# Rotary embedding on one core: a small zero write to the output, placed behind the load of batch 3

## The chip, the core and the metric

The kernel runs on one core of one Trainium2 chip. The metric is the device time of one execution in microseconds (us); lower is better. Three runs of the kernel before gave 317.55, 317.91 and 318.12 us, so its median is 317.91 us.

## What is computed

The reference applies a rotary position embedding. For each of 8 batches, 2048 positions and 16 heads, a row of 64 numbers is cut into two halves, which are rotated by the position's cosine and sine:

```python
x1 = x[..., :head_dim // 2].copy()
x2 = x[..., head_dim // 2:].copy()
...
out1 = x1 * cos - x2 * sin
out2 = x1 * sin + x2 * cos
return np.concatenate([out1, out2], axis=-1).astype(np.float32)
```

Input `x` and output have the shape (8, 2048, 16, 64) in float32, which is 8.39 MB for each batch and direction. `cos` and `sin` have 2048 rows of 32 numbers.

## The kernel before, in words

**Tiling.** One batch is one tile `xt` of 128 partitions with 16 positions (J = 16) of 16 heads of 64 numbers, so partition p holds positions 16p to 16p+15. In memory a partition's part of a batch is one contiguous piece of 64 KB. In SBUF the tile is float16 (32 KB a partition). The cast lies in the DMAs: `load` (L48) reads float32 and writes float16, `store` (L57) reads float16 and writes float32. Both are issued from GpSimd (POOL), and all of them go through one queue, q0 in the profile, in the order in which POOL issues them. I call the load of batch b "load b" and its store "store b".

**Buffers.** The pool `rope_io` has five buffers (NBUF, L27). Loads 0 to 4 are issued at once at the start (L74). Load 5 takes the buffer of batch 0 and waits until store 0 has landed; load 6 waits for store 1, and load 7 for store 2.

**Arithmetic.** `rotate` (L62) is four VectorE (DVE) instructions for each batch, at L67, L68, L70 and L72: two products into a scratch tile `v`, one product in place in `xt`, one sum in place. The store of a batch waits for its L72.

**Start.** The first two positions of batch 0 come in float32 through SyncE (SP) into `head` (L36), which the ScalarE (ACT) casts into the tile at L75. SP also loads `sin_f` (L45) and `cos_f` (L46), and ACT makes the float16 tables from them (L79, L80, L81). The DMAs from SP go through another queue, q1 in the profile.

**End.** The store of batch 7 is cut into three parts: 9 positions at L95 (`gate`), 5 positions at L97 (`rest`), both from POOL, and the last 2 positions through ACT's cast at L105 and a DMA from SP at L106, which waits for `gate` to land.

**What sets the order.** The program's scheduler puts POOL's DMAs in this order: loads 0 to 4, stores 0 and 1, loads 5 and 6, stores 2 and 3, load 7, stores 4, 5 and 6, `gate`, `rest`. POOL runs in order: when one of these waits, all that follow it wait. The ACT engine's order is L75, L79, L80, L81 and then, at the end of the kernel, L105. A helper, `add_manual_dep`, adds a dependency between two instructions by hand; with `Sync` the later one waits on a semaphore until the earlier one is done, and for a DMA this means that it has landed.

Of the kernel before, what the change touches and what calls it, by code (L numbers as in the profile page):

```python
# [1 line left out]

# [4 lines left out]


@with_exitstack  # L10
def kernel(
    ctx: ExitStack,
    tc: tile.TileContext,
    x: bass.AP,
    cos: bass.AP,
    sin: bass.AP,
    out: bass.AP,
):
    nc = tc.nc
    f16 = mybir.dt.float16  # L20
    f32 = mybir.dt.float32

    B, S, H, D = x.shape
    Dh = D // 2
    P = nc.NUM_PARTITIONS
    J = S // P
    NBUF = 5  # L27

    const_pool = ctx.enter_context(tc.tile_pool(name="rope_const", bufs=1))
    io_pool = ctx.enter_context(tc.tile_pool(name="rope_io", bufs=NBUF))  # L30
    tmp_pool = ctx.enter_context(tc.tile_pool(name="rope_tmp", bufs=1))

    JA = 2
    head = const_pool.tile([P, JA, H, D], f32)
    x0 = x[0].rearrange("(p j) h d -> p j (h d)", j=J)
    nc.sync.dma_start(  # L36
        out=head.rearrange("p j h d -> p (j h d)"),
        in_=x0[:, 0:JA, :].rearrange("p j f -> p (j f)"),
    )
    sin_f = const_pool.tile([P, J, Dh], f32)  # L40
    cos_f = const_pool.tile([P, J, Dh], f32)
    cos_h = const_pool.tile([P, J, Dh], f16)
    sin_h = const_pool.tile([P, J, Dh], f16)
    neg_h = const_pool.tile([P, J, Dh], f16)
    nc.sync.dma_start(out=sin_f, in_=sin.rearrange("(p j) d -> p j d", j=J))  # L45
    nc.sync.dma_start(out=cos_f, in_=cos.rearrange("(p j) d -> p j d", j=J))  # L46

    def load(b):  # L48
        xt = io_pool.tile([P, J, H, D], f16)
        j0 = JA if b == 0 else 0  # L50
        nc.gpsimd.dma_start(  # L51
            out=xt[:, j0:J, :, :].rearrange("p j h d -> p (j h d)"),
            in_=x[b].rearrange("(p j) h d -> p j (h d)", j=J)[:, j0:J, :].rearrange("p j f -> p (j f)"),
        )
        return xt

    def store(b, xt):  # L57
        nc.gpsimd.dma_start(  # L58
            out=out[b].rearrange("(p j) h d -> p (j h d)", j=J), in_=xt
        )  # L60

    def rotate(xt):  # L62
        v = tmp_pool.tile([P, J, H, D], f16)
        sin_b = sin_h.unsqueeze(2).to_broadcast([P, J, H, Dh])
        neg_b = neg_h.unsqueeze(2).to_broadcast([P, J, H, Dh])
        cos_b = cos_h.unsqueeze(2).to_broadcast([P, J, 2 * H, Dh])
        nc.vector.tensor_mul(out=v[:, :, :, 0:Dh], in0=xt[:, :, :, Dh:D], in1=neg_b)  # L67
        nc.vector.tensor_mul(out=v[:, :, :, Dh:D], in0=xt[:, :, :, 0:Dh], in1=sin_b)  # L68
        xw = xt.rearrange("p j h (e d) -> p j (h e) d", d=Dh)
        nc.vector.tensor_mul(out=xw, in0=xw, in1=cos_b)  # L70
        xa = xt.rearrange("p j h d -> p (j h d)")
        nc.vector.tensor_add(out=xa, in0=xa, in1=v.rearrange("p j h d -> p (j h d)"))  # L72

    tiles = [load(b) for b in range(NBUF)]  # L74
    nc.scalar.copy(  # L75
        out=tiles[0][:, 0:JA, :, :].rearrange("p j h d -> p (j h d)"),
        in_=head.rearrange("p j h d -> p (j h d)"),
    )
    nc.scalar.copy(out=sin_h, in_=sin_f)  # L79
    nc.scalar.mul(out=neg_h, in_=sin_f, mul=-1.0)  # L80
    nc.scalar.copy(out=cos_h, in_=cos_f)  # L81
    def part(b, j0, j1):
        return (
            out[b].rearrange("(p j) h d -> p j (h d)", j=J)[:, j0:j1, :].rearrange("p j f -> p (j f)"),
            tiles[b][:, j0:j1, :, :].rearrange("p j h d -> p (j h d)"),
        )

    for b in range(B):
        rotate(tiles[b])
        if b < B - 1:  # L90
            store(b, tiles[b])
        if b + NBUF < B:
            tiles.append(load(b + NBUF))
    dst, src = part(B - 1, 0, 9)
    gate = nc.gpsimd.dma_start(out=dst, in_=src)  # L95
    dst, src = part(B - 1, 9, J - JA)
    rest = nc.gpsimd.dma_start(out=dst, in_=src)  # L97
    tc.add_manual_dep(
        rest.ins,
        gate.ins.name,  # L100
        mybir.DependencyInfo(mybir.DependencyClass.NoSync, mybir.DependencyReason.DATA),
        reason="order of the ring",
    )
    dst, src = part(B - 1, J - JA, J)
    nc.scalar.copy(out=head.rearrange("p j h d -> p (j h d)"), in_=src)  # L105
    end = nc.sync.dma_start(out=dst, in_=head.rearrange("p j h d -> p (j h d)"))  # L106
    tc.add_manual_dep(
        end.ins,
        gate.ins.name,
        mybir.DependencyInfo(mybir.DependencyClass.Sync, mybir.DependencyReason.DATA),  # L110
        reason="the last rows go out behind this part",
    )


# [1 line left out]
_INS = ['x', 'cos', 'sin']  # L116
_OUTS = [((8, 2048, 16, 64), 'float32')]


# [23 lines left out]
```

## Time and profile before

| quantity | value |
|---|---|
| median of three runs | 317.91 us |
| time of the profiled execution | 317.42 us |
| its span, first to last instruction | 315.6 us |
| time outside of the span | 1.82 us |
| DVE busy | 209.2 us (66%) |
| ACT busy | 6.8 us (2%) |
| POOL busy | 9.4 us (3%) |
| read from HBM, written to HBM | 67.63 MB, 67.11 MB |

The table is from the page of the profiled execution. The span is the time from the first to the last instruction of the core; what lies outside of it is the difference between the profiled execution's own time and its span. A DMA's issue appears on the engine that issues it (POOLq and SPq are the sequencers' own rows) and takes about half a microsecond; the transfer itself runs later on the 16 DMA engines. Each DMA of 128 partitions appears there as 128 data packets, 8 for each DMA engine, and 16 packets of 4 bytes, one for each engine, which report completion. The profile counts a transfer by the bytes at its destination: a load of a batch counts 4.19 MB, a store 8.39 MB, though both have 8.39 MB on their HBM side.

### The profile page before, as it was taken

Reading aid. Unit: us, or ns where it says so; the run is one execution under the profiler, and the core shown is the slowest. Engines: PE = TensorE matmul, PEld = TensorE weight load, DVE = VectorE, ACT = ScalarE, POOL = GpSimd, SP = SyncE. Lnnn points to the kernel's source line nnn. Section 1 sums busy time; section 2 is a strip of 40 time slices with the busy share of each in tenths; the row PEclk is TensorE's granted clock in tenths of the full one; section 3 lists DMA queues with packets and bytes.
Section 4 is the critical chain, followed back from the end, with each engine's and each line's share of the span. In section 5 each row is a group of like instructions: output and inputs, shape, how many; then the busy total and the mean of one; then the engine's idle time right before and its main releaser. Section 6 shows DMA issues by size and latency. Waiting matters only on the chain.

```text
span 315.6 us, 126 instructions
## 1 busy us (share of the span) xinstructions
DVE 209.2 (66%) x32; ACT 6.8 (2%) x6; POOL 9.4 (3%) x21
## 2 busy tenths in 40 slices
DVE  0009599999999999999979999990009994000000
ACT  4010000000000000000000000000000002000000
POOL 3000000000000000010000000100000001000000
DMA  9899999999999999999999999999999999999998
GB/s 278 184 261 207 200 249 216 199 199 249 216 199 266 399 424 507 399 332 233 233 199 199 390 407 399 399 532 266 199 224 507 399 399 498 432 399 399 432 424 341
DMA packets 3024, 101.71 MB, mean 322 GB/s; under 512 B 336, under 2 KB 336, under 8 KB 592
## 3 DMA queue, kind: packets, MB, share of 16 engines
q0 software_dynamic: 2448, 99.09, 98.0%
q1 hardware_dynamic: 576, 2.62, 2.2%
HBM read 67.63 MB, written 67.11 MB: 427 GB/s over the span
## 4 chain that ended last, share of the span: by engine, by line
issue 25%; DMA 23%; DVE 21%; another core or an unknown queue 13%; POOL 1%; ACT 1%; SPq 0%; POOLq 0%; DVEq 0%; ACTq 0%
DMA xt<-in_x_dram 12%; DMA cos_f<-in_cos_dram 11%; DVE xt L70 8%; DVE xt L72 8%; DVE v L68 3%; DVE v L67 1%; ACT head L105 1%; POOL out_dram L58 1%; POOL xt L51 0%; ACT cos_h L81 0%; SPq L45 0%; SPq L36 0%; POOLq L58 0%; DVEq L67 0%
## 5 line engine op out<-in xcount | busy, mean ns | idle before, releaser
L70 DVE TENSOR_TENSOR xt<-xt,cos_h 128x16384 f16<-128x16384 f16 x8 | 69.5, 8692 | 4.2 <-ACT cos_h L81 3.9
L72 DVE TENSOR_TENSOR xt<-xt,v 128x16384 f16<-128x16384 f16 x8 | 69.5, 8692 | 0.3
L67 DVE TENSOR_TENSOR v<-xt,neg_h 128x8192 f16<-128x8192 f16 x8 | 35.4, 4425 | 50.1 <-DMA xt<-in_x_dram 49.9
L68 DVE TENSOR_TENSOR v<-xt,sin_h 128x8192 f16<-128x8192 f16 x8 | 35.3, 4417 | 0.0
L51 POOL DMA_DIRECT2D xt<-in_x_dram x8 | 4.4, 560 | 117.1 <-DMA out_dram<-xt 116.3
L105 ACT CAST head<-xt 128x2048 f32<-128x2048 f16 x1 | 1.9, 1897 | 227.6 <-DVE xt L72 227.6
L58 POOL DMA_DIRECT2D out_dram<-xt x7 | 3.7, 535 | 87.8 <-DVE xt L72 87.8
L95 POOL DMA_DIRECT2D out_dram<-xt x1 | 0.5, 531 | 50.5 <-DVE xt L72 50.5
L75 ACT CAST xt<-head 128x2048 f16<-128x2048 f32 x1 | 1.9, 1898 | 3.4 <-DMA head<-in_x_dram 3.4
L75 ACT ACT_TABLE_LOAD x1 | 1.3, 1283 | 0.7 <-PEq L127 0.7
L81 ACT CAST cos_h<-cos_f 128x512 f16<-128x512 f32 x1 | 0.6, 617 | 18.0 <-DMA cos_f<-in_cos_dram 18.0
L79 ACT CAST sin_h<-sin_f 128x512 f16<-128x512 f32 x1 | 0.6, 617 | 9.1 <-DMA sin_f<-in_sin_dram 9.1
L80 ACT ACTIVATE neg_h<-sin_f 128x512 f16<-128x512 f32 x1 | 0.6, 624 | 0.0
L97 POOL DMA_DIRECT2D out_dram<-xt x1 | 0.5, 531 | 0.0
L127 POOL MEMSET const-float32-0.0<- 128x1 f32 x1 | 0.1, 98 | 0.2 <-issue 0.2
L127 POOL MEMSET const-bfloat16-1.0<- 128x1 bf16 x1 | 0.1, 101 | 0.0
L127 POOL MEMSET const-float32-1.0<- 128x1 f32 x1 | 0.1, 98 | 0.0
L127 POOL MEMSET const-uint8-127<- 128x1 uint8 x1 | 0.1, 98 | 0.0
## 6 DMA issues: line engine op xcount, KB each, us to landing
xt<-in_x_dram POOLq DMA_DIRECT2D x7, 4096.0 KB, 41.1
out_dram<-xt POOLq DMA_DIRECT2D x1, 4608.0 KB, 42.3
xt<-in_x_dram POOLq DMA_DIRECT2D x1, 3584.0 KB, 22.2
out_dram<-xt POOLq DMA_DIRECT2D x1, 2560.0 KB, 47.9
head<-in_x_dram SPq DMA_DIRECT2D x1, 1024.0 KB, 4.7
out_dram<-head SPq DMA_DIRECT2D x1, 1024.0 KB, 8.4
sin_f<-in_sin_dram SPq DMA_DIRECT2D x1, 256.0 KB, 15.2
cos_f<-in_cos_dram SPq DMA_DIRECT2D x1, 256.0 KB, 33.9
```

The lines of the kernel that those rows point to most:

```text
L51: nc.gpsimd.dma_start(out=xt[:, j0:J, :, :].rearrange("p j h d -> p (j h d)"), in_=x[b].rearrange("(p j) h d -> p j (h d)", j=J)[:, j0:J, ...
L58: nc.gpsimd.dma_start(out=out[b].rearrange("(p j) h d -> p (j h d)", j=J), in_=xt)
L67: nc.vector.tensor_mul(out=v[:, :, :, 0:Dh], in0=xt[:, :, :, Dh:D], in1=neg_b)
L68: nc.vector.tensor_mul(out=v[:, :, :, Dh:D], in0=xt[:, :, :, 0:Dh], in1=sin_b)
L70: nc.vector.tensor_mul(out=xw, in0=xw, in1=cos_b)
L72: nc.vector.tensor_add(out=xa, in0=xa, in1=v.rearrange("p j h d -> p (j h d)"))
L75: nc.scalar.copy(out=tiles[0][:, 0:JA, :, :].rearrange("p j h d -> p (j h d)"), in_=head.rearrange("p j h d -> p (j h d)"),)
L79: nc.scalar.copy(out=sin_h, in_=sin_f)
L80: nc.scalar.mul(out=neg_h, in_=sin_f, mul=-1.0)
L81: nc.scalar.copy(out=cos_h, in_=cos_f)
L95: gate = nc.gpsimd.dma_start(out=dst, in_=src)
L105: nc.scalar.copy(out=head.rearrange("p j h d -> p (j h d)"), in_=src)
```

## The change

A tile of 128 partitions with 128 float32 zeros each (512 bytes) is made with a memset on POOL. A DMA that the ACT queue issues writes it to the output: in each partition's 64 KB piece of batch 0, to the first 512 bytes. By a dependency made by hand the DMA waits until load 3 has landed. Store 0 later writes the same bytes with the result. Since both write to the same place, the tile framework orders them. The built program's list of waits shows it: in it, store 0 waits for the DMA from ACT to land, besides the waits that it had before. In that program the memset stands on POOL behind loads 0 to 4 and ahead of store 0, and the DMA stands on ACT behind the cast of `cos_h` and ahead of the cast of L105 (L119 in the changed file). The order of all other instructions on each engine is the same.

```diff
@@ -45,13 +45,16 @@
+    loads = []
+
     def load(b):
         xt = io_pool.tile([P, J, H, D], f16)
         j0 = JA if b == 0 else 0
-        nc.gpsimd.dma_start(
+        dma = nc.gpsimd.dma_start(
             out=xt[:, j0:J, :, :].rearrange("p j h d -> p (j h d)"),
             in_=x[b].rearrange("(p j) h d -> p j (h d)", j=J)[:, j0:J, :].rearrange("p j f -> p (j f)"),
         )
+        loads.append(dma)
         return xt
@@ -79,6 +82,17 @@
     nc.scalar.copy(out=cos_h, in_=cos_f)
+    zero = const_pool.tile([P, 128], f32)
+    nc.gpsimd.memset(zero, 0.0)
+    blank = nc.scalar.dma_start(
+        out=out[0].rearrange("(p j) h d -> p (j h d)", j=J)[:, 0:128], in_=zero
+    )
+    tc.add_manual_dep(
+        blank.ins,
+        loads[3].ins.name,
+        mybir.DependencyInfo(mybir.DependencyClass.Sync, mybir.DependencyReason.DATA),
+        reason="a first write behind this load",
+    )
```

## The prediction, made before the changed kernel was run

> **What bounds the kernel now.** I read the page first: the busy shares, the row of DMA in 40 slices, and the queues.
>
> ```profile
> DVE 209.2 (66%) x32; ACT 6.8 (2%) x6; POOL 9.4 (3%) x21
> ...
> DMA  9899999999999999999999999999999999999998
> ...
> q0 software_dynamic: 2448, 99.09, 98.0%
> ...
> HBM read 67.63 MB, written 67.11 MB: 427 GB/s over the span
> ```
>
> No compute engine is the bound: DVE is busy for 66% of the span. The 16 DMA engines are busy in every slice, and POOL's queue q0 alone takes 98.0% of their time. So the end is set by one stream of transfers without a gap. A gap made anywhere in it moves everything behind it, and nothing later can take it back.
>
> Second I read the timeline around the place that is changed, for what is issued when.
>
> ```profile
> 0.74 0.38 SPq L36 DMA_DIRECT2D head<-in_x_dram  x1
> ...
> 1.25 2.79 POOL L51 DMA_DIRECT2D xt<-in_x_dram  x5 [0.80 <-PEq L138]
> ...
> 35.55 0.62 ACT L81 CAST cos_h<-cos_f 128x512 f16<-128x512 f32 x1 [17.98 <-DMA cos_f<-in_cos_dram]
> ...
> 54.18 0.54 POOL L58 DMA_DIRECT2D out_dram<-xt  x1 [50.14 <-DVE xt L72]
> ...
> 80.15 0.54 POOL L58 DMA_DIRECT2D out_dram<-xt  x1 [25.43 <-DVE xt L72]
> ...
> 121.83 0.53 POOL L51 DMA_DIRECT2D xt<-in_x_dram  x1 [41.14 <-DMA out_dram<-xt]
> ```
>
> Store 0 is issued at 54.18, store 1 at 80.15. Third, the DMA view of two short windows, one around the issue of load 3 (2.95) and one around that of load 4 (3.47), gives the time to landing:
>
> ```profile
> xt<-in_x_dram POOLq DMA_DIRECT2D x1, 4096.0 KB, 78.8
> ```
> ```profile
> xt<-in_x_dram POOLq DMA_DIRECT2D x1, 4096.0 KB, 98.7
> ```
>
> Load 3 lands at 2.95 + 78.8 = 81.7, load 4 at 3.47 + 98.7 = 102.2. So store 0 stands in the queue 48 us before the loads are through, and follows load 4 without a pause: its first packets start at 101.47 to 101.85 in the packet records (101.66 in the middle).
>
> Fourth, the last packets of load 4. The DMA view of 95.7 to 98.1 us and that of 98.1 to 101.4 us hold one packet of 32 KB for each engine:
>
> ```profile
> q0 software_dynamic: 16, 0.52, 101.4%
> ```
> ```profile
> q0 software_dynamic: 16, 0.52, 99.5%
> ```
>
> The first share means 1.014 x 2.4 = 2.43 us for a packet, the second 0.995 x 3.3 = 3.28 us. The engines lose 0.85 us here, just ahead of the run's first write to HBM; no other q0 packet of the trace takes over 2.6 us. This is what a first write placed earlier could move.
>
> **What the Trainium skill says.** The page "DMA: Bandwidth & Descriptors" bears on this in four places.
> - Section "Queues, rings and completion order": each DMA engine takes turns between the queues that have work, one packet at a time. Between 7.2 and 23.4 us the trace agrees: the two queues finish as many packets as each other, though q1's are small, and `cos_f` takes 33.9 us to land.
>
> ```profile
> q0 software_dynamic: 144, 3.74, 107.1%
> q1 hardware_dynamic: 144, 0.26, 4.8%
> ```
>
>  At the end the trace does not: L106 is issued at 306.36, but from 306.4 to 311.5 us only q0 has packets, and q1's start at 311.55 when q0 is empty.
>
> ```profile
> q0 software_dynamic: 107, 2.19, 104.0%
> ```
>
>  A DMA that comes to a filled queue may thus also have to wait for what is in it.
> - Section "Specifications": about 1 us to the first byte for a DMA from GpSimd, 0.6 us for one from SP or ACT. For SP the trace has 1.0 us (L36 at 0.74, first packets at 1.74). For POOL it has one case with an idle queue, the start: issue at 1.25, first q0 packet at 5.10, 3.85 us, which may be long because five issues stand together and `head` is on the engines.
> - Section "Anatomy of one DMA — SWDGE (gpsimd) path": a wait for a semaphore is done by the issuing sequencer before dispatch. The trace agrees: L51 at 121.83 follows the landing of store 0 (54.18 + 67.4 = 121.6) by 0.28 us.
> - Section "Issuing engines are not separate DMA queues": the ACT queue has no engines of its own. Here the SP queue's packets are on the same 16.
>
> **The change, part by part.**
> 1. *Memset on POOL.* 128 elements a partition behind the five load issues. The memsets of one element take 0.1 us; I take 0.1 to 0.3 us near 4 us. POOL then has nothing to do until 54.18. Cost 0. Without that cover it would be the 0.1 to 0.3 us.
> 2. *The wait on ACT.* ACT stands at the DMA from 36.2 (end of L81) until load 3 lands at 81.7. Behind it on ACT there is only the cast for the tail, which ran at 263.77, and nobody else waits for that. Cost 0; the cover is 180 us long.
> 3. *The zeros' transfer.* Issue about 81.8, ready for the engines 1.0 us later (the measured lead of L36), at 82.8. Load 4 has just begun, with 8 packets for each engine from 81.1 on, 2.43 us each. The zeros are also 8 packets for each engine. If the queues take turns, the first goes behind load 4's first packet, the eighth behind its eighth, at 102.1. A 2 KB packet of `sin_f` stretched the time from one load packet to the next from 2.13 to 2.21, so 512 bytes cost about 0.03 us each, 0.25 us in all. If the zeros must wait for what is queued, as at the tail, they start when load 4 ends. Either way they end when load 4 ends.
> 4. *The 0.85 us stall.* Taking turns, it comes under one of load 4's early packets, as long as before: no gain, and load 4 still ends at about 101.9. Waiting behind load 4, the load ends 0.85 us sooner and the zeros pay the stall: the same sum. At best it is hidden: minus 0.85. At worst it is paid by the zeros and by store 0 again: plus 0.85. I take 0.
> 5. *When the zeros have landed.* The last packet of a store ends 0.42 us before the landing is seen (store 0: completion packets up to 121.13, landing 121.55). That gives 102.1 + 0.42 = 102.5 with turns, and 102.7 without (101.0 + 0.85 + 8 x 0.05 + 0.42). I take 102.6.
> 6. *The new wait on store 0.* POOL reacts 0.28 us after a landing: issue at 102.9. From a POOL issue to its first packet the cost is 1.0 us by the skill, 3.85 us by the start of this trace. I take 1.8, which lies nearer the lower end because here one DMA is issued into idle engines. First packet at 104.7. Before, it was at 101.66. The gap is 3.0 us, from 2.2 to 5.1 by the lead alone. The first packets of `head` on idle engines took 0.43 to 0.94 instead of 0.31 us, so I add 0.1: 3.1 us.
> 7. *What stands behind store 0 on POOL.* Store 1, ready at 79.87, is issued half a microsecond behind it at about 103.4, far ahead of its turn at 124. Load 5 waits for the landing of store 0, while store 1 is on the engines for 19.3 us, so there is no second gap. Load 6, stores 2 and 3, load 7 and the rest follow in the same way, each 3.1 us later. DVE's wait ahead of batch 5 grows from 1.59 to 4.7 us, and its 209.2 us still fit.
>
> Sum: 0 + 0 + 3.1 = 3.1 us. From the profiled execution's own time, 317.42 + 3.1 = 320.5 us (span 318.7). The median of the runs lies 0.49 us above that execution, and I forecast on its scale: 317.91 + 3.1 = 321.0 us.
>
> **The rivals.**
> - *The zeros land early.* If an engine takes several of the 512-byte packets in one turn, four or more at once, they land before about 99. Store 0's issue (0.28 + 1.8 us) is then done before load 4 ends, and no gap opens. The point is 99.5: landing before it costs nothing. Place: inside load 4. If the 0.85 us stall is then hidden under load 4's reading, the time is 317.91 - 0.85 = 317.1, faster; if it holds load 4 up, 317.9. For it: the packets are small. Against it: `sin_f` and `cos_f` got one packet a turn, and the tail's DMA not even that.
> - *The lead of a POOL issue into idle engines is that of the start.* 102.9 + 3.85 = 106.8, and store 0 pays the 0.85 us as well: 5.1 + 0.85 = 6.0, hence 323.9 us. For it: the only idle start in the trace. Against it: five issues stood together there.
> - *The change doesn't do what it says*, because store 0 is not held back at run time, say because all semaphores are up before: 317.9. Against it: the list of waits of the built program has store 0 waiting on the landing of the zeros.
>
> **How the numbers follow.** Forecast 0.80 (time 319.2 to 323.2: from lead 1.0 with the stall hidden, 2.2 - 0.85, about +1.3, to lead 3.85, about +5.2). Early landing 0.10, half of it faster. Lead and stall both full 0.07. No effect 0.03. The range of 319.0 to 323.2 leaves out early landing, no effect and most of the third case, just under 2 in 10. A measurement of this kernel can tell about 0.2%, or 0.64 us, from no change. Faster: 0.05. Same: the other half of early landing and no effect, 0.08. Slower: 0.87.
>
> **What would show it.** Store 0's issue must move from 54.18 to about 102.9, with POOL's wait ahead of it ended by the DMA of the zeros, and store 1's must follow at once. The DMA row must have a hole of 2 to 5 us at 102 to 105, the only one. The stall of 3.28 us must move off load 4's last packet. Load 5 must be issued at about 125 instead of 121.83, and all after it shifted by the same amount. If store 0 is issued before 99, steps 3 and 6 are wrong; if the hole is there but the span does not grow by it, step 7 is.

## The result, and the profile after

The changed kernel takes 319.49 us in the median (318.87 to 319.90, 6 runs) against 317.94 us for the kernel before (317.36 to 318.12, 6 runs). The ratio is 1.0052 with a 95% interval of 1.0037 to 1.0067: slower by 1.55 us, where 3.1 were forecast. The profiled execution took 319.21 us with a span of 317.4 us; the spans differ by 1.8 us.

From the page of the kernel after, the lines that answer to those shown of before:

```profile
DVE 209.2 (66%) x32; ACT 6.8 (2%) x6; POOL 9.6 (3%) x22
...
DMA  9899999999996999999999999999999999999998
...
q0 software_dynamic: 2448, 99.09, 97.2%
...
q10 hardware_dynamic: 144, 0.07, 0.1%
HBM read 67.63 MB, written 67.17 MB: 425 GB/s over the span
```

The row of DMA has one new digit, a 6 in the 13th slice (95.2 to 103.2 us). Everything else is as full as before. q10 is the ACT queue: 128 data packets and 16 completion packets, 0.07 MB, 0.1% of the engines' time. What it moves takes next to nothing of the engines' time; what is new beside it is the hole.

The timeline of after around that slice, and the row of its view of waits that is new (engine, line, what it waited for: us in total, times, longest):

```profile
81.99 0.37 ACTq L87 DMA_DIRECT2D out_dram<-zero  x1
...
102.40 1.06 POOL L61 DMA_DIRECT2D out_dram<-xt  x2 [98.14 <-DMA out_dram<-zero]
...
123.67 0.53 POOL L53 DMA_DIRECT2D xt<-in_x_dram  x1 [20.20 <-DMA out_dram<-xt]
```
```profile
POOL out_dram L61 <- DMA out_dram<-zero: 98.1, 1, 98.1
```

The zeros are issued at 81.99, when load 3 has landed. Store 0 is issued at 102.40 in place of 54.18, released by the zeros, with store 1 right behind it. Load 5 is issued at 123.67 in place of 121.83, 1.84 us later, and that shift stays until the end. The windows view of after shows the hole (columns: the stretch, its length, busy time of DVE, ACT and POOL, clock, DMA share, GB/s):

```profile
98.00:100.00 2.00, 2.00 (x1) 0.00 (x0) 0.00 (x0) 1.00 1.24 266
100.00:102.00 2.00, 2.00 (x1) 0.00 (x0) 0.00 (x0) 1.00 0.04 9
102.00:104.00 2.00, 2.00 (x1) 0.00 (x0) 1.06 (x2) 1.00 1.22 524
104.00:106.00 2.00, 2.00 (x1) 0.00 (x0) 0.00 (x0) 1.00 0.99 426
```

A packet is counted where it starts, so a share over 1 reaches into the stretch behind it, and the hole lies from about 101 to 103.5 us. In the packet records load 4's data ends at 100.8 to 101.3, the zeros' last packets at 101.36, and store 0's first packets start at 103.51. The DMA view of 98.2 to 100.8 us has load 4's last packets:

```profile
q0 software_dynamic: 16, 0.52, 93.9%
q10 hardware_dynamic: 16, 0.01, 1.5%
```

0.939 x 2.6 = 2.44 us a packet: the stall of 0.85 us, which the kernel before has here and which I call "the loss" from here on, is gone, and no other load packet of after takes over 2.65 us. So the trace has two opposite terms. Means over 16 packets, one for each engine: load 4's last packets start at 98.54 (before: 98.36), so their usual 2.43 us end at 100.97; store 0's first start at 103.57 (before: 101.64). 2.60 us of gap, less 0.85 us of loss, plus 0.18 us by which load 4 is later, are the 1.93 us between 101.64 and 103.57.

### The profile page after: what moved, and what is told of

Its sections match the earlier page's. It is cut to its first block, busy times and chain, and to the rows that moved or that the text cites. A ratio compares the mean times of both kernels' runs of the same rounds, so it can differ in the third digit from the quotient of the medians.

```text
span 317.4 us, 131 instructions
## 1 busy us (share of the span) xinstructions
DVE 209.2 (66%) x32; ACT 6.8 (2%) x6; POOL 9.6 (3%) x22
## 4 chain that ended last, share of the span: by engine, by line
DMA 36%; issue 25%; another core or an unknown queue 14%; DVE 7%; ACT 1%; POOL 1%; SPq 0%; POOLq 0%; ACTq 0%; DVEq 0%
DMA xt<-in_x_dram 12%; DMA cos_f<-in_cos_dram 11%; DMA out_dram<-xt 7%; DMA out_dram<-zero 6%; DVE xt L75 3%; DVE xt L73 3%; DVE v L71 1%; ACT head L119 1%; POOL xt L53 0%; POOL out_dram L61 0%; ACT cos_h L84 0%; SPq L45 0%; SPq L36 0%; DVE v L70 0%
## 5 line engine op out<-in xcount | busy, mean ns | idle before, releaser
L70 DVE TENSOR_TENSOR v<-xt,neg_h 128x8192 f16<-128x8192 f16 x8 | 35.4, 4425 | 52.4 <-DMA xt<-in_x_dram 52.2
L119 ACT CAST head<-xt 128x2048 f32<-128x2048 f16 x1 | 1.9, 1897 | 229.4 <-DVE xt L75 229.4
```

## The experiments

Two things were open: why the loss of 0.85 us went away, and whether the gap is made as the prediction says. In all times, "before" is the kernel before, timed beside the experiment on the same chip. The lengths of packets are means over the 16 packets, one for each engine, of the one profiled execution.

**The zeros to another batch (e1_batch4).**

```diff
-        out=out[0].rearrange("(p j) h d -> p (j h d)", j=J)[:, 0:128], in_=zero
+        out=out[4].rearrange("(p j) h d -> p (j h d)", j=J)[:, 0:128], in_=zero
```

> The zeros go to the rows of batch 4 in place of batch 0, still behind load 3; store 0 is free of them, and store 4, which overwrites them, is issued 100 us after they land. My theory (the 0.85 us belong to the run's first write to HBM, and a small write takes them over unseen; the loss of the change is the gap of 2.15 us ahead of store 0): no gap, no packet of load 4 over 2.6 us, 317.1 us, about 0.8 us faster than before. Rival (the 0.85 us belong to the pass from loads to stores in a filled queue, and went away only because the queue was empty): no gap, load 4's last packet again 3.3 us, 317.9 us, as before.

317.71 us, before 317.79; ratio 0.9999 (0.9990 to 1.0007). Store 0 is issued at 51.96, the gap is gone, and with it the whole cost of the change. But load 4's last packets are long again, in the DMA view of 98.4 to 101.4 us:

```profile
q0 software_dynamic: 16, 0.52, 100.2%
```

1.002 x 3.0 = 3.01 us a packet. My theory fell: the zeros did not take the loss over.

**The zeros early (e2_load1).**

```diff
-        loads[3].ins.name,
+        loads[1].ins.name,
```

> As the change, with the zeros behind load 1 in place of load 3. They should land at 62 to 66 us and store 0 be issued then, 35 us before load 4 ends. First-write theory: no gap, no long packet, 317.1 us. Filled-queue rival: no gap, load 4's last packet 3.3 us, 317.9 us. A third view, in which it's the ACT queue itself that costs (a further queue to set up or to wait for at the end): over 318 us without any gap.

317.77 us, before 317.79; ratio 0.9998 (0.9991 to 1.0006). All 128 rows of zeros landed at 67.7, store 0 was issued at 68.28, no gap, and load 4's last packets are still long, in the DMA view of 98.6 to 101.4 us:

```profile
q0 software_dynamic: 16, 0.52, 104.1%
```

1.041 x 2.8 = 2.91 us a packet. So the loss doesn't belong to the run's first write to HBM, nor to the first write to these pieces of batch 0. The ACT queue itself costs nothing that can be measured, and neither does the wait on store 0 when it ends this early.

**No zeros, store 0 held until load 4 has landed (e3_hold).**

```diff
+            if b == 0:
+                tc.add_manual_dep(
+                    put.ins,
+                    loads[4].ins.name,
...
```

> No zeros; store 0 waits by hand for load 4 to land. This makes the gap without an early write. Both: load 4's last packet 2.43 us, landing about 101.3, issue about 101.9, first packets about 103.0. First-write theory: store 0 itself is then held up by about 0.85 us (long first packets or a landing that late), so the span grows by 2.2 us to about 317.8, 320.1 us. Filled-queue rival: no stall, the span grows by 1.4 us, 319.3 us.

318.77 us, before 317.79; ratio 1.0030 (1.0018 to 1.0041), 0.98 us slower. The timeline of e3_hold:

```profile
101.90 1.07 POOL L61 DMA_DIRECT2D out_dram<-xt  x2 [97.86 <-DMA xt<-in_x_dram]
```

Load 4's last packets took 2.43 us; store 0's first packets started at 103.07 in the mean and took 2.43 us, too. In both kernels in which store 0 comes to an empty queue, with the zeros and without, it pays no loss. The gap alone makes this kernel slower. It costs less than in the changed kernel, as load 4 lands at 101.32 here and the zeros land at 101.81 there, so store 0 is issued 0.50 us earlier.

**One packet for each engine in place of eight (e4_16rows).**

```diff
-        out=out[0].rearrange("(p j) h d -> p (j h d)", j=J)[:, 0:128], in_=zero
+        out=out[0].rearrange("(p j) h d -> p (j h d)", j=J)[0:16, 0:128], in_=zero[0:16, :]
```

> As the change, but only 16 of the 128 rows of zeros are written, so each DMA engine has one packet in place of eight. If the eight turns of one packet each are what carries the landing to 101.8, the zeros land at about 86.5 now, store 0 is issued at 87 and the gap is gone. First-write theory: 317.1 us. Filled-queue rival: 317.9 us. If the landing is set by something else than the turns, the gap stays and the time is near 319.5 us.

317.83 us, before 317.79; ratio 1.0001 (0.9992 to 1.0010). The timeline of e4_16rows, and the DMA view of its 97.9 to 101.3 us:

```profile
82.30 0.37 ACTq L87 DMA_DIRECT2D out_dram<-zero  x1
91.73 1.07 POOL L61 DMA_DIRECT2D out_dram<-xt  x2 [87.47 <-DMA out_dram<-zero]
```
```profile
q0 software_dynamic: 17, 0.52, 99.5%
```

The turns are what carries the landing: in the packet records the zeros' data start at 85.9 on 14 engines and at 88.4 on two, the completion packets one load packet later, at 88.4 and 90.8. They land at 91.1. I had expected 86.5, since I had counted neither the completion packet's own turn nor that two engines might join a packet later. There is no gap, but the loss is back (3.38 us in the mean; the 17th packet in the view is a completion packet of 4 bytes), though store 0 was issued as late as 91.73.

**The kernel before again (e5_before).** No edit.

> The kernel before, once more, for a second profile. If the loss ahead of store 0 belongs to the kernel and not to one execution, load 4's last packets are long again, by 0.5 to 0.95 us (the four cases so far: 0.85, 0.62, 0.49, 0.96), and no other load shows it. If it was chance, it is gone or lies elsewhere.

Load 4's last packets took 3.17 us. The loss is there in both profiles of the kernel before.

**A gap at a later pass from loads to stores (e6_hold2).** The kernel before; store 3 also keeps its place behind store 2.

```diff
+            if b == 2:
+                tc.add_manual_dep(
+                    put.ins,
+                    loads[6].ins.name,
...
```

> The kernel before, with a gap made at a later pass from loads to stores: store 2 waits for load 6 to land, store 3 follows it. At that pass the kernel before loses nothing (load 6's last packets 2.43 us). Landing about 179.4, issue 180.0. View A (the lead of 1.1 us from POOL's issue to the first packet is that of any issue into idle engines, and the loss ahead of store 0 vanishes in an empty queue): first packets 181.1, 2.2 us later than before, 320.0 us. View B (store 0's loss lay inside its lead of 1.1 us in the two kernels with a gap): first packets here at 180.3 to 180.5, 1.4 us later, 319.2 us.

319.51 us, before 317.46; ratio 1.0065 (1.0053 to 1.0078), 2.05 us slower. The timeline of e6_hold2, and its DMA view of 179.2 to 180.8 us:

```profile
179.85 1.06 POOL L61 DMA_DIRECT2D out_dram<-xt  x2 [38.27 <-issue]
```
```profile
DMA packets 0, 0.00 MB, mean 0 GB/s; under 512 B 0, under 2 KB 0, under 8 KB 0
```

The timeline names no releaser for store 2; load 6 landed at 179.31, 0.54 us ahead of the issue. Store 2's first packets start at 181.02 in the mean, 1.2 us behind the issue, and 2.24 us later than load 6's packets would have let them. View A holds: the lead of 1.1 to 1.2 us is there at a store without a loss, too, so store 0's loss does not hide in it. Where no loss is taken back, the drained queue costs 2.05 us. The loss ahead of store 0 is still there in this kernel (3.41 us).

**A small first store on POOL's own queue (e7_q0_zeros).** The kernel before.

```diff
-    tiles = [load(b) for b in range(NBUF)]
+    zero = const_pool.tile([P, 128], f16)
+    nc.vector.memset(zero, 0.0)
+    tiles = [load(b) for b in range(3)]
+    nc.gpsimd.dma_start(
+        out=out[4].rearrange("(p j) h d -> p (j h d)", j=J)[:, 0:128], in_=zero
+    )
+    tiles += [load(b) for b in range(3, NBUF)]
```

> The kernel before, and POOL itself writes float16 zeros to the rows of batch 4 between loads 2 and 3, with a cast as the stores have it: the first store of this queue is then small and early. View C (the loss belongs to the first store that the queue itself carries, whatever its size): the packets ahead of the zeros, near 60 us, are long by 0.5 to 0.9 us, and load 4's last ones are not; 317.8 us, or up to 0.7 us less if the small store hides it. View D (it belongs to the first large store): load 4's last packets stay long, 317.9 us.

317.34 us, before 317.46; ratio 0.9998 (0.9989 to 1.0006). The packets ahead of the small store are as short as ever, load 4's last took 3.18 us: view D.

**64 rows of zeros (e8_64rows), and again (e12_64rows).**

```diff
-        out=out[0].rearrange("(p j) h d -> p (j h d)", j=J)[:, 0:128], in_=zero
+        out=out[0].rearrange("(p j) h d -> p (j h d)", j=J)[0:64, 0:128], in_=zero[0:64, :]
```

> As the change, with 64 rows of zeros: four data packets and one completion packet for each DMA engine in place of eight and one. By one packet a turn they land at 96 to 99, store 0 is issued 0.6 us later, and its first packet can start 1.1 us after that, at or just ahead of load 4's end near 101.2. Gap 0 to 0.5 us. If a store that comes to a filled queue pays the loss, load 4's last packets are long and the time is 317.8 us; if such a late one does not, 317.1 to 317.4 us.

> The kernel of e8_64rows again, beside the two kernels with a mark: does its gain hold? Expected 0.9 us less than before, no long packet, no gap.

316.58 us, before 317.46; ratio 0.9973 (0.9962 to 0.9983). The second time 316.56 us, before 317.45; ratio 0.9972 (0.9961 to 0.9983). This is faster than both kernels. The timeline of e8_64rows, and the DMA view of its 97.9 to 100.5 us:

```profile
81.92 0.53 ACTq L87 DMA_DIRECT2D out_dram<-zero  x1
99.48 1.07 POOL L61 DMA_DIRECT2D out_dram<-xt  x2 [95.23 <-DMA out_dram<-zero]
```
```profile
q0 software_dynamic: 16, 0.52, 93.5%
q10 hardware_dynamic: 6, 0.00, 0.3%
```

The zeros land at 98.9. Store 0, issued at 99.48, can start 1.1 us later at 100.6, just when load 4 ends. Its first packets start at 100.73 in the mean, without a gap, and load 4's last packets took 0.935 x 2.6 = 2.43 us. In the second run the picture is the same: issue at 99.16, load 4's last packets 2.43 us, store 0's first packets at 100.68 behind load 4's end at 100.67. My reading is that half the zeros serve as a timer only, which lets store 0 in late enough to pay no loss and early enough to leave no gap. The next two runs were to test it without zeros.

**The moment alone, without zeros (e9_mark97 and e11_mark88).** The kernel before, with stores 0 and 1, and with them loads 5 and 6, set behind a product of batch 2: the third one (L70) in e9_mark97, the second one (L68) in e11_mark88.

```diff
+    def first_stores(mark):
+        put = store(0, tiles[0])
+        tc.add_manual_dep(
+            put.ins,
+            mark.ins.name,
...
```

> The kernel before, without any zeros; store 0 waits by hand for the third product of batch 2 (end 97.4 us), store 1 follows it. Issue at 97.7, first packet possible at 98.8, when most engines have begun load 4's last packet (98.2 to 98.5). My theory now (the loss comes only if store 0 stands in the queue before load 4's last packets begin; a store that comes in the last 2.4 us is met without loss and without a gap): no packet over 2.6 us, no gap, 0.85 us less than before, 316.7 to 317.0 us. Rival (the zeros had a part in what e8_64rows gained): load 4's last packets long as before, no change.

> The same kernel, but store 0 waits for the second product of batch 2 (end 88.6 us): issue near 89, in the queue four packets ahead of load 4's end. Only the moment differs from e9_mark97. Theory: the loss is back, load 4's last packets 3.0 to 3.4 us, no change against before. If it is gone here too, the moment is not what counts, but the order or the new wait.

e11_mark88: 317.46 us, before 317.45; ratio 0.9999 (0.9991 to 1.0007). e9_mark97: 317.37 us, before 317.45; ratio 0.9993 (0.9986 to 0.9999). The timelines, e9_mark97 first, then e11_mark88:

```profile
95.83 1.07 POOL L58 DMA_DIRECT2D out_dram<-xt  x2 [91.80 <-DVE xt L70]
```
```profile
89.65 1.07 POOL L58 DMA_DIRECT2D out_dram<-xt  x2 [85.61 <-DVE v L68]
```

The DMA views of 97.8 to 101.3 us, in the same order:

```profile
q0 software_dynamic: 16, 0.52, 99.2%
```
```profile
q0 software_dynamic: 16, 0.52, 98.1%
```

Both profiles have the loss (0.992 x 3.5 = 3.47 us and 0.981 x 3.5 = 3.43 us). For e9_mark97 the mark did not hit the moment: in its profiled execution `cos_f` landed at 33.4, and not at 35.5, so DVE ran 2 us ahead and store 0 was in the queue at 96.9, before load 4's last packets began (97.9 to 98.6). Its 22 times run from 316.26 to 317.75, seven of them at 316.95 or less, under the lowest of before (317.23); those of e11_mark88 from 317.32 to 317.76. That fits a mark that falls now on one side of the moment, now on the other. It is an inference, as only one execution has a trace. So it is not shown that the moment alone, without any zeros, takes the loss away.

**A large first store earlier (e10_early_large).** The kernel before.

```diff
+    early = nc.gpsimd.dma_start(
+        out=out[4].rearrange("(p j) h d -> p (j h d)", j=J)[0:16, JA * H * D :],
+        in_=tiles[0][0:16, JA:J, :, :].rearrange("p j h d -> p (j h d)"),
+    )
...
```

> The kernel before, and POOL writes 16 partitions of batch 0's loaded tile (56 KB each, one large packet for each DMA engine) to the rows of batch 4 between loads 2 and 3; store 4 overwrites them. It costs about 2.2 us of engine time in any case, so 319.7 us at least. If the loss belongs to the first large store of the queue, the packets ahead of it near 62 us are long by 0.5 to 0.9 us and load 4's last are not: 319.7 to 320 us. If it belongs to the pass from load 4 to store 0, load 4's last are long: 319.7 us or a little above, too. The long packets decide, not the time. Loads 3 and 4 are issued at 24 us here, not at 4.

318.80 us, before 317.45; ratio 1.0044 (1.0032 to 1.0056). The DMA view of its 58.9 to 61.7 us, the packets ahead of the early store:

```profile
q0 software_dynamic: 16, 0.52, 96.8%
```

0.968 x 2.8 = 2.71 us, a loss of 0.28 us. The DMA view of 100 to 102.6 us has load 4's last packets, and one completion packet:

```profile
q0 software_dynamic: 17, 0.52, 93.6%
```

0.936 x 2.6 = 2.43 us, though store 0 was issued at 83.08 and stood in the queue for some 20 us. So there is no loss ahead of store 0 here, and a smaller one ahead of the early store. As that store went to rows of batch 4, the loss is not tied to the first large write to batch 0's rows. The time missed what I had expected (319.7 us at least), since the loss did not move in full: 2.13 us for the early packet + 0.28 - 0.85 = 1.56, measured 1.35 us. Not separated: loads 3 and 4 are issued at 24.7 and 25.3 us here, and DVE's L70 of batch 0 waits for the early store (it starts at 65.08 in place of 36.20), so store 0 comes 29 us later. That a late issue alone doesn't do it, e4_16rows and e11_mark88 show.

## Why the prediction came out as it did

The mechanism was right: the zeros end with load 4, store 0 is issued too late, one hole opens, and the rest moves by it. The wait is the cause: with the same zeros and no wait on store 0 the cost is gone (e1_batch4), with a wait that ends early, too (e2_load1, e4_16rows), and a wait without zeros brings a cost back (e3_hold). Two terms were too large.

- Steps 1 and 2 (memset, wait on ACT) were right: the memset took 0.26 us at 4.0, and the ACT queue without the wait on store 0 costs nothing (e1_batch4).
- Step 3 was right in its end and wrong in its count. The zeros took turns, but joined at 85.97, one packet later than I had it, and the completion packet takes a turn of its own (e4_16rows). A turn went to one packet record, so to one row of zeros. So three of the nine turns were left when load 4's data ended, and ran in under 0.1 us on each engine. The landings with one, four and eight rows for each engine (91.1, 98.9 and 101.81 us) show that the number of turns sets the landing.
- Step 4 failed. I took 0 for the loss of 0.85 us, as it would come under load 4 or in the gap. It came nowhere: store 0 didn't pay it in an empty queue (after, e3_hold), and it doesn't hide in the lead (e6_hold2). I had tied it to the first write to HBM, and e2_load1 refutes that. Gain: 0.85 us, the best case that the step named.
- Step 5: the landing was 101.81, not 102.6. These 0.79 us are nearly all step 4's loss.
- Step 6 had the right form and a wrong size. From landing to issue it took 0.59 us and not 0.28, which was read at a load (L51); the stores of e3_hold and e6_hold2 that wait for a landing took 0.58 and 0.54 us, and why a store reacts later than a load stays open. From issue to first packet 1.11 us and not 1.8. Together 1.70 in place of 2.08 us. The first packets took 2.43 us, so the 0.1 us for a slow start was not needed.
- Step 7 was right in its form: load 5 came 1.84 us later, the end 1.8 us, and no second gap opened. DVE's wait ahead of batch 5 grew from 1.59 to 3.44 us and cost nothing.

In the sum, first packets at 103.57 in place of 104.7 and no 0.1 us: 3.1 us became 1.93 us in the trace and 1.55 us in the medians. The time lies near the lower end of the forecast range, which stood for a lead of 1.0 us with the loss hidden, about +1.3 us. That is the case that came about, while the point stood on another, at twice the cost. That the range held is owed to its width and not to the point.

Of the rivals, the early landing missed only by its number of packets. Its limit for a free landing, 99.5, agrees with the one run near it: at 98.89 (e8_64rows) there was no gap. Its gain came about there, but not because the zeros took the loss over: they leave it in e1_batch4, e2_load1 and e4_16rows. The start's lead of 3.85 us did not show again: three emptied queues (after, e3_hold, e6_hold2) gave 1.1 to 1.2 us.

Shown: the gap and its price; that a small write beforehand, from ACT's or POOL's queue, leaves the loss; that it is absent when store 0 can start as load 4's last packets end (from 100.3 and 100.6 us by the lead of 1.1 us, e12_64rows and e8_64rows, both with zeros), or later. Where between 96.9 us (e9_mark97, with the loss) and 100.3 us the limit lies was not measured; that it lies where load 4's last packets begin, I only inferred. One run, with other differences in it, has a smaller loss ahead of an earlier large store and none ahead of store 0. What in the hardware makes the loss stays open.

## What to carry to other kernels

When one filled queue of transfers sets the end, a wait put on one of its DMAs is free only if it ends before the queue runs dry by at least the time from landing to first packet, here 1.7 us. When it ended later it cost up to 2.05 us here (e6_hold2), which nothing later gave back. A small DMA from another engine did not land quickly beside the large packets of the loads: it took one turn for each of its packets on a DMA engine, and one for the completion, here 2.43 us each. So cut the number of its packets, or keep anything urgent from waiting for it. This is shown beside loads; beside the last stores of the kernel before, L106's DMA had no packet for 5.2 us, and no run here shows why. And look for terms of opposite sign: here the 1.55 us of the medians hide a gap of 2.60 us and a loss of 0.85 us that went away.

## What the runs showed of the hardware that was not expected

- **A loss that comes once, at the first pass from loads to large stores.** Nine profiles in which store 0 was queued before load 4's last packets began show it, from 0.48 to 1.04 us (before, e1, e2, e4, e5, e6, e7, e9, e11). The tenth, e10_early_large, has 0.28 us ahead of its early store instead. At the later passes, behind loads 5, 6 and 7, the last packets took 2.43 us in every profile.
- **A small write beside stores may be held up long after its data.** In e1_batch4 the zeros' last data packets ended at 104.34, but they landed only at 82.52 + 39.8 = 122.3:

```profile
DMA to landing us min/median/max: 39.8/39.8/39.8
```

 Its completion packets, begun at 104.0 to 106.7, lasted 14.5 to 16.9 us, to the end of store 0 (landing 122.43). The Trainium skill's page "DMA: Bandwidth & Descriptors", section "Queues, rings and completion order", says that a completion lands only after every earlier write of that DMA engine, across its queues. The run agrees in that a write of another queue held the completion up. But the wait is longer than the writes under way explain: 16.9 us are seven times the 2.41 us from one of store 0's packets to the next, and these seven began with the completion packets or after them. Store 0 as a whole had been issued earlier, at 51.96; whether that is what counts was not tested. In the changed kernel store 0 is issued only after the zeros have landed, so no store stands beside their completion packets, which took 0.01 us.
